# A new order for the splits at the border between the value product and the attention heads

## The chip, the cores and the metric

The kernel runs on one core of a Trainium2 chip. The metric is device time in microseconds (us), lower is better; the time of a kernel is the median of its timed runs. TensorE (PE) multiplies matrices, VectorE (DVE), ScalarE (ACT) and GpSimd (POOL) work on rows of 128 partitions, and SyncE (SP) issues the transfers from device memory.

## The reference

Two residual layers over 512 frames of 1024 channels, all in float32. Layer 0 mixes by causal pooling, layer 1 by chunked attention with 16 heads of 64 channels; each is followed by a gated MLP of width 2816 with a causal convolution. What matters here is the attention of layer 1, cut to its core:

```python
qkv = h @ w_qkv
q, k, v = jnp.split(qkv, 3, axis=-1)
q = head_rmsnorm(q.reshape(B, S, N_HEADS, HEAD_DIM), q_norm)
k = head_rmsnorm(k.reshape(B, S, N_HEADS, HEAD_DIM), k_norm)
...
s = jnp.einsum('bqhd,bkhd->bhqk', qc, kb) * scale + bias
s = jnp.where(valid, s, -1e30)
p = jax.nn.softmax(s, axis=-1)
o = jnp.einsum('bhqk,bkhd->bqhd', p, vb)
return o @ w_o
```

## The kernel before

Every float32 product is made of three products of a rounded "hi" part and the "lo" rest of each operand: hi by hi, hi by lo, lo by hi. So each operand is split first: ScalarE rounds a tile to its hi part (`nc.scalar.activation(hi, raw, AF.Copy)`), and VectorE, or GpSimd for some weights, subtracts (`lo = raw - hi`).

`opening` is the first part of attention. It computes the query and key columns of the first four pairs of heads (`query`), and then the values V (512 frames by 1024 channels) by a scheme of seven block products in place of eight (Strassen's). Each of the seven has two halves, `half(0)` to `half(13)`; half n multiplies by a weight block whose parts are made by `hi(n)` (ScalarE, line 990) and `lo(n)` (VectorE, line 993). The results gather in banks of PSUM: the pair A (tiles `va0`, `va1`, in the Q banks), the pair B of the last block product but one (`vd0`, `vd1`, in the P banks), and C (`vc0`, `vc1`). Quadrants of V are sums over these banks: `add(y5, C)` and `add(y6, B)` (line 1162, two VectorE additions of 128x512 each) and, for the last, plain copies of A into `c` (`c120` on ScalarE, `c121` on VectorE). `store` then scales a finished tile of V by the norm of its frames and splits it into the tiles `one`: four ScalarE instructions (line 107) and four VectorE instructions (line 108), each 128x128.

Behind the values stands `project(1)`, the query and key columns of the next four pairs: four groups of 24 matmuls, one group for each weight tile `wqk1_0` to `wqk1_3`, each matmul triple going to one of four banks in turn. Its tiles `qk1_0` and `qk1_1` lie in the P banks, where B was, and `qk1_2` and `qk1_3` in the Q banks, where A was. So its first triple may start when `vd0` was added up, the seventh matmul when `c120` was copied, and the tenth when `c121` was copied. The first weight tile is loaded and split ahead (`then`, the split lines `nc.scalar.activation(then[0], ...)` and `nc.vector.tensor_sub(then[1], ...)`); the lo parts of the other three (`wqk1_1_l` to `wqk1_3_l`) are made by GpSimd (line 103), and their hi parts by ScalarE (line 102).

The heads follow: `scores`, `turn` and `mix` for 16 heads by four frame tiles, with the matmuls of `project` and of the output product as fillers between them.

What sets the order: in `opening` the order of PE, VectorE, ScalarE and SP is the order in which the code stands (a manual schedule). GpSimd's order, and the order of VectorE, ScalarE and SP in the heads, come from a scheduler that works with a cost model; PE's order there is written out too. Each engine works off its queue in order, so an instruction that waits holds all that stand behind it on that engine.

Of the kernel before, what the change touches and what calls it, by code (L numbers as in the profile page):

```python
# [72 lines left out]
def trunk(ctx: ExitStack, tc: tile.TileContext, xt, xT, cols, band, edge, poolw, gv, wout, wqk, wv, wo, rel, out):  # L73
# [15 lines left out]
    def psum(tag, name, bufs=2):  # L89
        return ps.tile([P, S], F32, name=name, tag=tag, bufs=bufs)  # L90
# [3 lines left out]
    def g_tile(name):  # L94
        return tmp.tile([P, S], F32, name=name, tag="g", bufs=6)
# [9 lines left out]
    def split_scaled(src, scale, hi, lo):  # L105

        nc.scalar.activation(hi, src, AF.Copy, scale=scale)
        nc.vector.scalar_tensor_tensor(lo, src, scale, hi.bitcast(F32), op0=OP.mult, op1=OP.subtract)
# [24 lines left out]
    def rsqrt(a, y, t):  # L133

        nc.scalar.activation(t, a, AF.Ln)
        seed = nc.scalar.activation(y, t, AF.Exp, scale=-0.5)
        nc.vector.scalar_tensor_tensor(t, y, -0.5, y, op0=OP.mult, op1=OP.mult)
        nc.vector.tensor_mul(t, t, a)
        return seed, nc.vector.scalar_tensor_tensor(y, t, 1.5, y, op0=OP.add, op1=OP.mult)
# [775 lines left out]
    def attention(rest, hook, hidden_slots):  # L915
# [8 lines left out]
        def norms_of(c):  # L924
            return [big.tile([P, 8 * TT], F32, name=f"qk{c}_{v}", tag="nw", bufs=4) for v in "sayt"]

        def by_frame(v):
            return v.rearrange("p (t h) -> p t h", t=TT)
# [3 lines left out]
        def opening(pre):  # L932
# [55 lines left out]
            def part_hi(key):  # L988
                part[key] = [wp.tile([P, 1024], F32R, name=f"{key}_{c}", tag=f"w{c}", bufs=2) for c in "hl"]
                nc.scalar.activation(part[key][0], raws[key], AF.Copy)  # L990

            def part_lo(key):
                nc.vector.tensor_sub(part[key][1], raws[key], part[key][0].bitcast(F32))
# [25 lines left out]
            def hi(n):  # L1019
                z, j = divmod(n, 2)  # L1020
                raws[f"v{n}"] = blocks[SEQ[z], j]
                part_hi(f"v{n}")

            def lo(n):
                part_lo(f"v{n}")
# [57 lines left out]
            def half(n, o, name, first):  # L1083
                z, j = divmod(n, 2)
                h, l = part.pop(f"v{n}")
                how = {"skip_group_check": not first}
                for c in range(2):
                    s = slice(c * S, (c + 1) * S)
                    for i in range(2):
                        sh, sl = stationary(name, 2 * j + c, i)  # L1090
                        nc.tensor.matmul(o[i], sh, h[:, s], start=first and n % 2 == 0 and c == 0, stop=False, **how)
                        nc.tensor.matmul(o[i], sl, h[:, s], start=False, stop=False, **how)
                for i in range(2):
                    for c in range(2):
                        sh, _ = stationary(name, 2 * j + c, i)
                        nc.tensor.matmul(o[i], sh, l[:, c * S:(c + 1) * S], start=False, stop=j == 1 and c == 1, **how)
# [63 lines left out]
            def add(x, o):  # L1160
                for i in range(2):
                    nc.vector.tensor_add(x[i], x[i], o[i])

            def store(src, t, h):
                for hh in range(2):
                    V[t, 2 * h + hh] = vt = set1[(t * 2 + h) * 2 + hh].rearrange("p (h a d) -> p h a d", h=4, a=2)
                    v4 = src[:, hh * 256:(hh + 1) * 256].rearrange("p (h d) -> p h d", d=HD)
                    for e in range(2):
                        split_scaled(v4[:, e::2, :], rcol[:, t:t + 1], vt[:, e::2, e, :], vt[:, e::2, 1 - e, :])

            def pair_of(name):
                return [vx(f"{name}{i}") for i in range(2)]
# [26 lines left out]
            B = [psum("P", f"vb{i}") for i in range(2)]  # L1199
# [22 lines left out]
            y6 = pair_of("y6")  # L1222
# [23 lines left out]
            y5 = pair_of("y5")  # L1246
# [3 lines left out]
            B = [psum("P", f"vd{i}") for i in range(2)]  # L1250
# [3 lines left out]
            hi(12)  # L1254
            lo(12)
            add(y5, C)
            store(y5[0], 2, 1)
            half(11, B, "a22", True)
            hi(13)
            lo(13)  # L1260
            nc.scalar.activation(then[0], raw, AF.Copy)
            add(y6, B)
            nc.vector.tensor_sub(then[1], raw, then[0].bitcast(F32))
            half(12, A, "s4", False)
            store(y5[1], 3, 1)
            half(13, A, "s4", False)
            c = pair_of("c12")
            nc.scalar.activation(c[0], A[0], AF.Copy)
            nc.vector.tensor_copy(c[1], A[1])  # L1269
            second = project(1, ready=then)  # L1270
            for _ in range(24):
                next(second)
# [6 lines left out]
        def products(ov, w, name, eng=None, evict=None, ready=None):  # L1279

            for kk in range(4):
                hi, lo = ready if ready and kk == 0 else load_split(w[kk], 1024, f"{name}_{kk}", eng=eng)

                for c, t in [(c, t) for c in range(2) for t in range(TT)] if kk < 3 else [(c, t) for t in range(TT) for c in range(2)]:
                    k = 2 * kk + c
                    s = slice(c * S, (c + 1) * S)
                    q = slice(t * P, (t + 1) * P)
                    yield from mm3(ov[t], XS[k][:, q], XS[KD + k][:, q], hi[:, s], lo[:, s], k == 0, k == KD - 1)
                    if kk == 3 and c and evict:
                        evict(t)  # L1290

        def project(c, banks="PQ", ready=None):

            ov = [psum(banks[t // 2], f"qk{c}_{t}", BANKS[banks]) for t in range(TT)]
            ss, a, y, t_ = norms_of(c)
            s3, a3, y3 = (by_frame(v) for v in (ss, a, y))

            def squares(t):
                sq = g_tile(f"zs{c}_{t}")
                nc.scalar.activation(sq, Z[c, t].rearrange("p h d -> p (h d)"), AF.Square)  # L1300
                nc.vector.tensor_reduce(s3[:, t, :], sq.rearrange("p (h d) -> p h d", d=HD), axis=mybir.AxisListType.X, op=OP.add)


            def evict(t):
                Z[c, t] = z = zp.tile([P, 8, HD], F32, name=f"z{c}_{t}", tag="z", bufs=8)
                flat = z.rearrange("p h d -> p (h d)")
                if t % 2:
                    nc.vector.tensor_copy(flat, ov[t])
                else:
                    nc.scalar.activation(flat, ov[t], AF.Copy)  # L1310
                late.append(lambda: squares(t))

            yield from products(ov, wqk[c], f"wqk{c}", nc.gpsimd, evict, ready)

            def norms():
                nc.vector.tensor_mul(a3, s3, r2[:, :, None].to_broadcast([P, TT, 8]))
                nc.vector.tensor_scalar(a, a, EPS, None, op0=OP.add)
                rsqrt(a, y, t_)
                nc.vector.tensor_mul(y3, y3, rcol[:, :, None].to_broadcast([P, TT, 8]))
                for t in range(TT):  # L1320
                    nc.gpsimd.tensor_mul(Z[c, t], Z[c, t], y3[:, t, :, None].to_broadcast([P, 8, HD]))

            late.append(norms)
# [105 lines left out]
        with tc.tile_pool(name="pre", bufs=1, reuse_waits="tile") as pre:  # L1429
            with tc.manual_schedule(engines={ET.PE, ET.DVE, ET.Activation, ET.SP}):  # L1430
                rcol, second = opening(pre)
# [147 lines left out]
```

## Time and profile before

| | before |
| --- | --- |
| median of 3 runs | 969.64 us |
| runs | 969.39 to 969.65 us |
| the profiled execution | 969.34 us |
| its span | 967.5 us |
| PE busy | 957.4 us, 99% of the span |
| VectorE busy | 850.8 us, 88% |
| ScalarE busy | 593.7 us, 61% |
| GpSimd busy | 94.6 us, 10% |

The border lies at 430 to 450 us of the span. Rows of the timeline read: start, duration, engine, line, operation, what is written from what, how many, and in brackets how long the engine stood idle before it and what ended that. Successive instructions of an engine overlap a little, so the step from one start to the next is shorter than the duration. Buffer numbers are left out of names: `y` is any of y50 to y61, `one` any of the tiles of V, `wqk_l` any lo part.

### The profile page before, as it was taken

What the parts mean: (1) busy time and instruction counts of PE and PEld (TensorE: products, weight loads), DVE (VectorE), ACT (ScalarE), POOL (GpSimd) and SP (SyncE); (2) the same over time, 40 slices, a digit from 0 to 9 for tenths busy, and PEclk for the clock granted to TensorE, in tenths of its full rate; (3) what the DMA queues carried; (4) which work ended last, traced back from release to release, by engine and by line L of the source; (5) the groups of instructions that cost most, each with busy time, mean ns of one, the idle gap of its engine ahead of it and who ended that gap; (6) DMA issues with size and microseconds to landing.
All of it is one profiled execution on the core that took longest, in us unless ns stands there. A gap on an engine that the chain in (4) does not pass through costs nothing.

```text
span 967.5 us, 13741 instructions
## 1 busy us (share of the span) xinstructions
PE 957.4 (99%) x4958; PEld 810.7 (84%) x4958; DVE 850.8 (88%) x1521; ACT 593.7 (61%) x1023; POOL 94.6 (10%) x82
## 2 busy tenths in 40 slices
PE   8999999999999999999999999999999999999998
PEld 7788988888888888887888787888988888888886
DVE  8999999999899859895777887999999999989953
ACT  7665554655555457465898988646565565456531
POOL 2300000000000000033435442000000000000000
PEclk9999999999999999999999999999999999999999
DMA  8222332332323317024443341232333233332323
GB/s 344 75 95 71 115 111 78 120 120 81 115 78 120 103 52 290 18 66 130 121 119 99 92 119 55 100 109 80 94 114 111 80 120 111 102 102 80 113 80 111
DMA packets 38996, 103.87 MB, mean 107 GB/s; under 512 B 4464, under 2 KB 7936, under 8 KB 38928
## 3 DMA queue, kind: packets, MB, share of 16 engines
q1 hardware_dynamic: 38864, 102.95, 32.8%
q8 instruction: 39, 0.64, 0.3%
q14 instruction: 29, 0.24, 0.1%
q0 software_dynamic: 32, 0.04, 0.0%
q10 hardware_dynamic: 32, 0.00, 0.0%
HBM read 96.65 MB, written 2.14 MB: 102 GB/s over the span
## 4 chain that ended last, share of the span: by engine, by line
PE 94%; DVE 3%; ACT 2%; issue 0%; DMA 0%; DVEq 0%
PE st_m L593 11%; PE out L124 8%; PE out L123 8%; PE out L125 8%; PE st_m L595 6%; PE st_t L593 6%; PE gv L124 4%; PE gv L123 4%; PE gv L125 4%; PE qk L123 3%; PE qk L124 3%; PE qk L125 3%; PE st_t L595 3%; PE st_b L593 3%; PE tp L1407 2%; PE oo L1419 2%
## 5 line engine op out<-in xcount | busy, mean ns | idle before, releaser
L124 PE MATMUL out<-one,ow_h 128*128 128x512 f32 x224 | 88.1, 393 | 0.0
L123 PE MATMUL out<-one,ow_h 128*128 128x512 f32 x224 | 88.0, 393 | 0.0
L125 PE MATMUL out<-one,ow_l 128*128 128x512 f32 x224 | 87.9, 393 | 0.0
L829 DVE TENSOR_TENSOR X<-out,X 128x512 f32<-128x512 f32 (+1 forms) x65 | 44.0, 678 | 46.3 <-PE out L125 46.1
L593 PE MATMUL st_m<-two,g_h 128*128 128x512 f32 x240 | 75.0, 394 | 0.0
L593 PE MATMUL st_m<-h,g_h 128*128 128x512 f32 x240 | 74.1, 390 | 0.0
L392 ACT ACTIVATE ow_h<-wo_r 128x768 fp32r<-128x768 f32 (+1 forms) x56 | 44.5, 794 | 43.2 <-PE out L124 40.6
L407 DVE SCALAR_TENSOR_TENSOR c<-a,col,c 128x511 f32<-128x511 f32 (+1 forms) x76 | 56.1, 740 | 0.0
L593 PEld LDWEIGHTS st_m<-h,g_h 128*128 128x128 f32 x240 | 45.1, 188 | 10.3
L595 PEld LDWEIGHTS st_m<-two,g_l 128*128 128x128 f32 x240 | 45.0, 188 | 9.6
L602 ACT ACTIVATE w<-st_m 128x512 f32<-128x512 f32 x30 | 17.9, 598 | 56.6 <-PE st_m L595 56.6
L593 PEld LDWEIGHTS st_m<-two,g_h 128*128 128x128 f32 x240 | 44.1, 188 | 10.1 <-ACT w L602 0.8
L393 DVE TENSOR_TENSOR ow_l<-wo_r,ow_h 128x768 fp32r<-128x768 f32 (+1 forms) x56 | 49.8, 890 | 2.1 <-ACT ow_h L392 2.1
L595 PE MATMUL st_m<-h,g_l 128*128 128x256 f32 x240 | 48.3, 283 | 0.0
L595 PE MATMUL st_m<-two,g_l 128*128 128x256 f32 x240 | 47.6, 280 | 0.0
L124 PEld LDWEIGHTS out<-one,ow_h 128*128 128x128 f32 x224 | 42.4, 189 | 5.6 <-DVE one L418 0.3
L125 PEld LDWEIGHTS out<-one,ow_l 128*128 128x128 f32 x224 | 42.4, 189 | 5.5
L123 PEld LDWEIGHTS out<-one,ow_h 128*128 128x128 f32 x224 | 42.4, 189 | 5.4
L404 ACT ACTIVATE c<-a,col 128x512 f32<-128x512 f32 x38 | 30.7, 813 | 23.6 <-DVE a L751 21.9
L1397 ACT ACTIVATE sb<-sb,mx 128x128 f32<-128x128 f32 (+1 forms) x64 | 35.7, 557 | 13.2 <-DVE mx L1395 12.8
L1395 DVE CUSTOM_DVE_ANT_0 sb<-sc,B 128x128 f32<-128x128 f32 (+1 forms) x64 | 31.1, 486 | 14.4 <-PE sc L1392 11.2
L123 PE MATMUL qk<-wqk_h,two 128*128 128x512 f32 x96 | 39.9, 416 | 1.7 <-DVE c L1269 1.7
(458 smaller groups left out, 3028.1 us busy)
## 6 DMA issues: line engine op xcount, KB each, us to landing
gv_r<-gv SPq DMA_DIRECT2D x86, 512.0 KB, 4.0
wo_r<-wout SPq DMA_DIRECT2D x32, 384.0 KB, 3.1
wo_r<-wout SPq DMA_DIRECT2D x32, 320.0 KB, 2.9
wqk_r<-wqk SPq DMA_DIRECT2D x12, 512.0 KB, 3.4
b<-wv SPq DMA_DIRECT2D x8, 512.0 KB, 6.6
wo_r<-wo SPq DMA_DIRECT2D x8, 512.0 KB, 3.4
xt<-xt SPq DMA_DIRECT2D x4, 512.0 KB, 5.2
X<-xT SPq DMA_DIRECT2D x8, 256.0 KB, 7.5
```

The costliest lines, as they stand in the source:

```text
L123: yield nc.tensor.matmul(o, sh, mh, start=first, stop=False, **how)
L124: yield nc.tensor.matmul(o, sh, ml, start=False, stop=False, **how)
L125: yield nc.tensor.matmul(o, sl, mh, start=False, stop=last, **how)
L392: nc.scalar.activation(hi[:, :n], raw[:, :n], AF.Copy)
L393: return hi, lo, lambda: nc.vector.tensor_sub(lo[:, :n], raw[:, :n], hi[:, :n].bitcast(F32))
L404: nc.scalar.activation(c, a, AF.Identity, scale=cw[2], bias=cw[3])
L407: nc.vector.scalar_tensor_tensor(c[:, j:], a[:, :S - j], cw[2 - j], c[:, j:], op0=OP.mult, op1=OP.add)
L593: nc.tensor.matmul(o, hi[:, c], B[i, name], start=first and i == 0, stop=False, **how)
L595: nc.tensor.matmul(o[:, 0], lo[:, c], B[i, name][:, 0], start=False, stop=i == 3, **how)
L829: nc.vector.tensor_add(X[d][:, fs], o[:, fs], X[d][:, fs])
L1395: nc.vector.tensor_tensor_reduce(out=s_[:, :n], in0=sc[:, :n], in1=BT[h % 2][:, :n][:, ::-1], scale=1.0, scalar=3e38, op0=OP.add, op1=OP.m ...
L1397: nc.scalar.activation(s_[:, :n], s_[:, :n], AF.Exp, scale=-1.0, bias=mx[:, 0:1], accum_out=mx[:, 1:2])
```

## The change

The same instructions are issued, in another order. `hi(13)` and the split of the first weight tile of `project(1)` come before the splits of y5, `add(y6, B)` comes before `lo(13)`, the splits of `y5[0]` come behind the split of that weight tile, and those of `y5[1]` behind the copies of the last bank into `c`.

```diff
             add(y5, C)
-            store(y5[0], 2, 1)
             half(11, B, "a22", True)
             hi(13)
+            add(y6, B)
             lo(13)
             nc.scalar.activation(then[0], raw, AF.Copy)
-            add(y6, B)
             nc.vector.tensor_sub(then[1], raw, then[0].bitcast(F32))
             half(12, A, "s4", False)
-            store(y5[1], 3, 1)
+            store(y5[0], 2, 1)
             half(13, A, "s4", False)
             c = pair_of("c12")
             nc.scalar.activation(c[0], A[0], AF.Copy)
             nc.vector.tensor_copy(c[1], A[1])
+            store(y5[1], 3, 1)
             second = project(1, ready=then)
```

VectorE from the sums of y5 to the copy of the last bank, before (`v13_l` is the lo part for half 13, `wqk1_0_l` that of the first weight tile, the tiles `one` are splits of V, `c121` the copy; x2 stands for two instructions):

```order
L1162 TENSOR_TENSOR y50_4140<-y50_4140,vc0_4027 128x512
L1162 TENSOR_TENSOR y51_4141<-y51_4141,vc1_4028 128x512
L108 SCALAR_TENSOR_TENSOR one10_90<-y50_4140,n1_y_3837,one10_90 128x2x64 x2
L108 SCALAR_TENSOR_TENSOR one11_91<-y50_4140,n1_y_3837,one11_91 128x2x64 x2
L993 TENSOR_TENSOR v13_l_4190<-b22r_1_4047,v13_h_4189 128x1024
L1162 TENSOR_TENSOR y60_4021<-y60_4021,vd0_4145 128x512
L1162 TENSOR_TENSOR y61_4022<-y61_4022,vd1_4146 128x512
L1263 TENSOR_TENSOR wqk1_0_l_4150<-wqk1_0_r_4147,wqk1_0_h_4149 128x1024
L108 SCALAR_TENSOR_TENSOR one14_94<-y51_4141,n1_y_3837,one14_94 128x2x64 x2
L108 SCALAR_TENSOR_TENSOR one15_95<-y51_4141,n1_y_3837,one15_95 128x2x64 x2
L1269 COPY c121_4230<-va1_3706 128x512
```

The same place on VectorE in the changed kernel:

```order
L1162 TENSOR_TENSOR y50_4140<-y50_4140,vc0_4027 128x512
L1162 TENSOR_TENSOR y51_4141<-y51_4141,vc1_4028 128x512
L1162 TENSOR_TENSOR y60_4021<-y60_4021,vd0_4145 128x512
L1162 TENSOR_TENSOR y61_4022<-y61_4022,vd1_4146 128x512
L993 TENSOR_TENSOR v13_l_4182<-b22r_1_4047,v13_h_4181 128x1024
L1262 TENSOR_TENSOR wqk1_0_l_4150<-wqk1_0_r_4147,wqk1_0_h_4149 128x1024
L108 SCALAR_TENSOR_TENSOR one10_90<-y50_4140,n1_y_3837,one10_90 128x2x64 x2
L108 SCALAR_TENSOR_TENSOR one11_91<-y50_4140,n1_y_3837,one11_91 128x2x64 x2
L1268 COPY c121_4222<-va1_3706 128x512
```

Ahead of the copy stand four splits of V where eight stood; the other four follow it. The sums of y6 stand ahead of `v13_l`.

ScalarE from the hi part for half 13 on, in the changed kernel (`wqk1_1_h` and `wqk1_2_h` are hi parts of the second and third weight tile, `sb0_0` the first softmax row of the heads):

```order
L990 ACTIVATE v13_h_4181<-b22r_1_4047 128x1024
L1261 ACTIVATE wqk1_0_h_4149<-wqk1_0_r_4147 128x1024
L107 ACTIVATE one10_90<-y50_4140,n1_y_3837 128x2x64 x2
L107 ACTIVATE one11_91<-y50_4140,n1_y_3837 128x2x64 x2
L102 ACTIVATE wqk1_1_h_4313<-wqk1_1_r_4312 128x1024
L1267 ACTIVATE c120_4221<-va0_3705 128x512
L107 ACTIVATE one14_94<-y51_4141,n1_y_3837 128x2x64 x2
L107 ACTIVATE one15_95<-y51_4141,n1_y_3837 128x2x64 x2
```

Before, the rows of `one10` and `one11` stood ahead of `v13_h`, and those of `one14` and `one15` ahead of `wqk1_1_h` and `c120`. After these come the splits of y6 and of `c`, 16 ScalarE instructions. `wqk1_2_h` stood ahead of the last four of them and stands behind all of them now, still ahead of the first softmax row. GpSimd takes the lo part of that tile two rows later, behind the two small memsets of the heads' tiles B:

```order
 L103 TENSOR_TENSOR wqk_1_l<-wqk_1_r,wqk_1_h 128x1024
-L103 TENSOR_TENSOR wqk_2_l<-wqk_2_r,wqk_2_h 128x1024
 L1436 MEMSET B_4306 64x64
 L1436 MEMSET B_4307 64x64
+L103 TENSOR_TENSOR wqk_2_l<-wqk_2_r,wqk_2_h 128x1024
```

Here `wqk_1_l` is `wqk1_1_l` and `wqk_2_l` is `wqk1_2_l`. The orders of PE and SP are unchanged.

## The prediction

> **What bounds the kernel now.** I read the busy times on the profile's page first, then the list of PE's waits over the whole span, and then the windows around the border.
>
> ```profile
> PE 957.4 (99%) x4958; PEld 810.7 (84%) x4958; DVE 850.8 (88%) x1521; ACT 593.7 (61%) x1023; POOL 94.6 (10%) x82
> ```
>
> ```profile
> PE qk L123 <- DVE c L1269: 1.7, 1, 1.7
> PE wo L124 <- DVE two L103: 0.6, 1, 0.6
> PE oo L1419 <- DVE pt1l L103: 0.5, 1, 0.5
> ```
>
> ```profile
> 420.00:440.00 20.00, 19.82 (x88) 15.69 (x86) 19.36 (x29) 16.00 (x36) 4.38 (x3) 1.00 0.42 125
> 440.00:460.00 20.00, 18.44 (x85) 15.35 (x86) 9.74 (x31) 9.11 (x23) 7.36 (x5) 1.00 0.35 111
> 460.00:480.00 20.00, 20.00 (x110) 16.81 (x109) 15.57 (x47) 17.29 (x42) 10.33 (x9) 1.00 0.40 111
> ```
>
> PE bounds the kernel, and its longest single wait of the span is at the border that the change touches: 1.7 us, ended by the VectorE copy into `c`. The columns of the windows are length, PE, PEld, DVE, ACT, POOL (busy us and instructions), clock, DMA share and GB/s. VectorE is full until 440 (19.36 of 20) and half empty after it (9.74 of 20), and from 460 PE is full again: what PE wins at the border should stay won, since VectorE catches up right behind it. The clock column is 1.00 on both sides of the stall.
>
> The timeline of PE shows the loss in full.
>
> ```profile
> 437.30 0.39 PE L123 MATMUL qk<-wqk_h,two 128*128 128x512 f32 x1
> 437.77 0.50 PE L124 MATMUL qk<-wqk_l,two 128*128 128x512 f32 x1
> 439.51 0.40 PE L125 MATMUL qk<-wqk_h,two 128*128 128x512 f32 x1
> 441.56 0.50 PE L123 MATMUL qk<-wqk_h,two 128*128 128x512 f32 x1 [1.66 <-DVE c L1269]
> 441.89 0.39 PE L124 MATMUL qk<-wqk_l,two 128*128 128x512 f32 x1
> 445.10 0.39 PE L123 MATMUL qk<-wqk_h,two 128*128 128x512 f32 x1
> 450.79 0.40 PE L123 MATMUL qk<-wqk_h,two 128*128 128x512 f32 x1
> ```
>
> These are matmuls 1, 2, 9, 10, 11, 25 and 49 of `project(1)`. From 11 to 25 the step is 3.21 / 14 = 0.229 us. Without any stall, matmul 11 would stand at 437.30 + 10 x 0.229 = 439.59; it stands at 441.89. So 2.30 us are lost: a little at matmul 2, which needs `wqk1_0_l`, and the rest at matmul 10, which needs the copy `c121`. **2.30 us is the most that the change can win here.**
>
> **Why the copy is late** is read from the VectorE timeline.
>
> ```profile
> 430.05 1.22 DVE L993 TENSOR_TENSOR v_l<-b22r,v_h 128x1024 fp32r<-128x1024 f32 x1
> 431.18 1.28 DVE L1162 TENSOR_TENSOR y<-y,vc 128x512 f32<-128x512 f32 x2
> 432.38 1.18 DVE L108 SCALAR_TENSOR_TENSOR one<-y,n_y,one 128x128 fp32r<-128x128 f32 x4
> 434.16 1.23 DVE L993 TENSOR_TENSOR v_l<-b22r,v_h 128x1024 fp32r<-128x1024 f32 x1 [0.59 <-ACT v_h L990]
> 435.30 1.28 DVE L1162 TENSOR_TENSOR y<-y,vd 128x512 f32<-128x512 f32 x2
> 436.50 1.22 DVE L1263 TENSOR_TENSOR wqk_l<-wqk_r,wqk_h 128x1024 fp32r<-128x1024 f32 x1
> 437.63 3.27 DVE L108 SCALAR_TENSOR_TENSOR one<-y,n_y,one 128x128 fp32r<-128x128 f32 x4
> 440.83 0.68 DVE L1269 COPY c<-va 128x512 f32<-128x512 f32 x1
> 441.43 4.32 DVE L108 SCALAR_TENSOR_TENSOR one<-y,n_y,one 128x128 fp32r<-128x128 f32 x8
> 445.68 2.18 DVE L108 SCALAR_TENSOR_TENSOR one<-c,n_y,one 128x128 fp32r<-128x128 f32 x8
> ```
>
> VectorE is behind by its own work, and it loses 0.59 us waiting for `v13_h`. The group of four splits at 437.63 took 3.27 us, the one at 432.38 only 1.18. Taken by line, one instruction of the slow group is the difference, and GpSimd was busy beside it:
>
> ```profile
> L108 DVE SCALAR_TENSOR_TENSOR one<-y,n_y,one x4: 340/340/2486, 437.6 to 440.6; 128x128 fp32r<-128x128 f32 x4
> 437.33 2.64 POOL L103 TENSOR_TENSOR wqk_l<-wqk_r,wqk_h 128x1024 fp32r<-128x1024 f32 x1 [13.84 <-PE va L1096]
> 442.21 2.61 POOL L103 TENSOR_TENSOR wqk_l<-wqk_r,wqk_h 128x1024 fp32r<-128x1024 f32 x1 [2.23 <-ACT wqk_h L102]
> 452.25 2.40 POOL L103 TENSOR_TENSOR wqk_l<-wqk_r,wqk_h 128x1024 fp32r<-128x1024 f32 x1 [7.01 <-ACT wqk_h L102]
> 460.57 0.68 DVE L1308 COPY z<-qk 128x512 f32<-128x512 f32 x1
> 460.35 0.61 POOL L1372 CAST z<-zh 64x512 fp32r<-64x512 f32 x1
> ```
>
> Three splits took 340 ns and one 2486 ns, from 437.63 to 440.12, when GpSimd's subtraction was through at 439.97. The same again from 442.21 to 444.82, where eight splits took 4.32 us instead of 2.18. Alone, at 452.25, GpSimd's subtraction takes 2.40. While GpSimd subtracts, a VectorE split does not advance. A VectorE copy out of PSUM does: at 460.57 it takes 0.68 us beside a busy GpSimd, as long as the copy at 440.83 alone.
>
> **The change, part by part.** No instruction is added or removed, so the sum is made of places in the queues. VectorE is unchanged up to 431.18. From there: sums of y5, 1.20 (431.18 to 432.38); sums of y6, 1.20 (435.30 to 436.50), so `v13_l` can start at 433.58; it takes 1.14 (434.16 to 435.30), so `wqk1_0_l` starts at 434.72 instead of 436.50, **1.78 us earlier**. That is the four splits of `y5[0]` moved behind (1.19) and the idle 0.59. Each start has to be allowed by others.
>
> ```profile
> 430.72 0.39 PE L1092 MATMUL vd<-v_h,two 128*128 128x512 f32 x1
> 430.95 1.07 PE L1096 MATMUL vd<-v_l,two 128*128 128x512 f32 x4
> 433.67 1.07 PE L1096 MATMUL va<-v_l,one 128*128 128x512 f32 x4
> 436.39 1.07 PE L1096 MATMUL va<-v_l,one 128*128 128x512 f32 x4
> 431.89 0.40 ACT L107 ACTIVATE one<-y,n_y 128x128 fp32r<-128x128 f32 x1 [2.45 <-DVE y L1162]
> 434.03 1.05 ACT L1261 ACTIVATE wqk_h<-wqk_r 128x1024 fp32r<-128x1024 f32 x1
> 434.98 1.26 ACT L107 ACTIVATE one<-y,n_y 128x128 fp32r<-128x128 f32 x4
> 436.15 1.05 ACT L102 ACTIVATE wqk_h<-wqk_r 128x1024 fp32r<-128x1024 f32 x1
> ```
>
> The sums of y6 read bank B, which PE closes at 430.95 + 1.07 = 432.02; they start at 432.38, so the wait that they add costs nothing, with 0.36 us to spare, and only VectorE's own row stands behind them. `v13_h` takes the buffer of `v11_h`, which PE reads last at 430.72 + 0.39 = 431.11. ScalarE idled 2.45 us until 431.89 and now makes `v13_h` from 431.15 to 432.2 and `wqk1_0_h` to 433.15, both ahead of need. PE's half 13 needs `v13_l`, through at 434.80, at 436.39 only: covered by 1.6 us.
>
> What remains is whether GpSimd's subtraction of `wqk1_1` still falls on splits ahead of the copy. It needs `wqk1_1_h` from ScalarE. That now stands behind the four splits of `y5[0]`, 433.05 to 434.3, and needs its transfer.
>
> ```profile
> 431.29 0.35 SPq L117 DMA_DIRECT2D wqk_r<-wqk  x1
> wqk_r<-wqk SPq DMA_DIRECT2D x1, 512.0 KB, 3.1
> ```
>
> Issued at 431.29 when `v12_l` is through, as before, and 3.1 us to landing: 434.4. So ScalarE splits the tile from 434.45 to 435.5, and GpSimd arrives at 435.6; its buffer has been free since PE's 433.67 + 1.07 = 434.74. Before, it arrived at 437.33, behind the hi part (436.15 + 1.05 = 437.20; the bracket names PE, one of whose matmuls ended in the same moment) and 0.83 us into VectorE's `wqk1_0_l` of 436.50; now 0.9 us into the same instruction, begun at 434.72. The whole pattern is moved as it stands: **GpSimd again falls on the four splits ahead of the copy**, which now belong to `y5[0]`. From the start of `wqk1_0_l` to the copy it was 440.83 - 436.50 = 4.33 us; so the copy starts at 434.72 + 4.33 = 439.05, and PE's matmul 10 follows 0.73 after it as before (441.56 - 440.83): 439.78, against 439.36 without any stall. Matmul 11 comes 0.33 later at 440.11 instead of 441.89. The small stall at matmul 2 goes too, since `wqk1_0_l` is through at 435.94, but that only lengthens the wait at matmul 10. **Sum: -1.78 us.**
>
> Bounds: the unknown is GpSimd's hold on VectorE ahead of the copy. If it falls elsewhere, four free splits take 1.19 us, the copy waits for PE alone (436.39 + 1.07 = 437.46), and all 2.30 us are won. If it gets in before `wqk1_0_l`, that lo part is through only at about 435.94 + 2.40 = 438.34, PE's matmul 2 waits for it from 437.53 to about 438.4, and matmul 11 stands at 438.4 + 9 x 0.229 = 440.5, later than by the copy: 1.4 us are won. I take 1.78, the row at hand.
>
> The Trainium skill, page "SBUF — State Buffer", section "Who interferes with whom", says that VectorE instructions with two inputs in SBUF and GpSimd instructions that read SBUF exclude each other, and whoever starts first holds the port for its whole instruction. Taken literally, GpSimd would run 2.40 us from the end of `wqk1_0_l` and the four splits only then, 435.94 + 2.40 + 1.19 = 439.53 for the copy, a gain of 1.30 us instead of 1.78. In this trace the blocked split ends 0.15 us behind GpSimd, and less than that time is lost.
>
> Behind the border: `wqk1_2_h` stands behind all ScalarE splits. From `c120` at 437.1 + 0.57 come 20 of them at 0.29 (1.17 for four, 434.98 to 436.15), to 443.5, so `wqk1_2_h` is ready at 444.5 and GpSimd's lo part at about 447.2, against 444.82 before. Matmul 49 and 50 need it, at 450.79 - 1.78 = 449.0 and 449.2. Margin 2.0 us: nothing. It blocks the last VectorE splits to about 447.6; the first scores are wanted after 448: nothing. The hi parts ahead of it on ScalarE serve V, first needed by `mix` much later.
>
> **The rivals.**
>
> A, GpSimd is out of the way and the stall goes whole: 969.64 - 2.30 = 967.3. For it: a copy out of PSUM isn't blocked, so a `wqk1_1_h` later by 1.3 us would do. Against: transfer and ScalarE row above leave it nothing to wait for.
>
> B, GpSimd's hold lasts longer or begins before `wqk1_0_l`: gain 1.3 to 1.4, 968.3. For it: the arrival is reckoned to 0.2 us only. Against: it cannot come before 434.74, and in the rows before the four splits were through 3.20 us after their start. The skill's rule above gives this time too.
>
> C, most of the gain is given back in the heads, by small waits there that double (0.6 at `wo`, 0.5 at `oo`): 969.64 - 1.78 + 1.1 = 969.0. Against: everything behind 441 follows PE, so those waits should move with it.
>
> D, on the other side: `wqk1_2` comes too late. If ScalarE's 20 splits went at VectorE's pace in the rows above (3.20 + 4.25 + 2.18 = 9.63 from one start to the next), `wqk1_2_h` would be through at 437.67 + 9.63 + 1.05 = 448.35; if then eight VectorE splits (2.18) also went ahead of GpSimd's 2.40, the lo part would be ready at 452.9, and PE would wait from 449.2: 969.64 - 1.78 + 3.7 = 971.6. It costs from 449.2 on, and is slower than before from 451.0. Against: ScalarE's four splits take 1.26 us and wait for no one in these rows.
>
> **How the numbers follow.** Forecast 0.62, A 0.20, B 0.08, C 0.06, D 0.04. The profiled execution would take 969.34 - 1.78 = 967.56 us; runs stand 0.3 above it, so the median is 969.64 - 1.78 = **967.86 us**. A measurement of this kernel tells a change from none at about 0.2%, 1.94 us, and the forecast lies just inside. Faster by more: nearly all of A and a third of the forecast's own scatter (small waits of a few tenths in the heads), 0.39; within: 0.57; slower: 0.04. The range takes in A and B with that scatter and reaches just past C: 966.9 to 969.2.
>
> **What would show it.** Right: the wait of PE at `qk` falls from 1.66 to about 0.3 us, the copy starts near 439.05, one split of `y5[0]` again lasts about 2.5 us, matmul 11 stands near 440.1, and 460 to 480 is full on PE. A shows no wait at `qk`, B one of `qk` for `wqk_l`, D one at matmul 49 or 50. Wrong altogether: a new wait of PE between 427 and 437, where half 11 to half 13 run without a gap now.

## The result

| | before | changed |
| --- | --- | --- |
| median of 12 runs | 969.64 us | 967.72 us |
| runs | 969.24 to 970.45 us | 967.46 to 968.66 us |
| profiled execution (span) | 969.34 (967.5) us | 967.76 (966.0) us |

The ratio is 0.9982, with a 95% interval of 0.9974 to 0.9989: 1.9 us faster, clear of no change by the interval, and just inside 0.2%. The forecast was 967.86.

PE's longest waits over the whole span, in the changed kernel:

```profile
PE warm L199 <- POOL ident masks.py:199: 1.4, 1, 1.4
PE y L278 <- ACT two L222: 1.0, 1, 1.0
PE wo L124 <- DVE two L103: 0.7, 1, 0.7
PE oo L1419 <- DVE pt1l L103: 0.5, 1, 0.5
...
PE qk L123 <- DVE c L1268: 0.4, 1, 0.4
```

The wait for the copy fell from 1.7 to 0.4 us. Those in the heads, at `wo` and `oo`, are what they were to 0.1 us (0.6 and 0.5 before). The wait at `warm`, ahead of the first matmul, is 1.4 us in both kernels. The wait at `y`, at the kernel's start and untouched, happened to be 1.0 us in this execution, against 0.6 in that of before; so the spans differ by 1.5 us only, and all times at the border stand some 0.2 us later than they would.

The timeline of PE in the changed kernel, matmuls 1, 2, 9, 10, 11 and 50 of `project(1)`:

```profile
437.49 0.39 PE L123 MATMUL qk<-wqk_h,two 128*128 128x512 f32 x1
437.72 0.39 PE L124 MATMUL qk<-wqk_l,two 128*128 128x512 f32 x1
...
439.31 0.39 PE L125 MATMUL qk<-wqk_h,two 128*128 128x512 f32 x1
440.05 0.50 PE L123 MATMUL qk<-wqk_h,two 128*128 128x512 f32 x1 [0.36 <-DVE c L1268]
440.39 0.39 PE L124 MATMUL qk<-wqk_l,two 128*128 128x512 f32 x1
...
449.51 0.39 PE L124 MATMUL qk<-wqk_l,two 128*128 128x512 f32 x1
```

A measure that does not depend on where the border stands in the span is the distance from matmul 1 to matmul 11: 441.89 - 437.30 = 4.59 us before, 440.39 - 437.49 = **2.90 us** after, and 2.29 at PE's own step. It is used for every experiment below.

VectorE, and below it ScalarE and GpSimd, in the same kernel:

```profile
431.45 1.28 DVE L1162 TENSOR_TENSOR y<-y,vc 128x512 f32<-128x512 f32 x2
432.64 1.28 DVE L1162 TENSOR_TENSOR y<-y,vd 128x512 f32<-128x512 f32 x2
433.83 1.23 DVE L993 TENSOR_TENSOR v_l<-b22r,v_h 128x1024 fp32r<-128x1024 f32 x1
434.97 1.22 DVE L1262 TENSOR_TENSOR wqk_l<-wqk_r,wqk_h 128x1024 fp32r<-128x1024 f32 x1
436.11 3.29 DVE L108 SCALAR_TENSOR_TENSOR one<-y,n_y,one 128x128 fp32r<-128x128 f32 x4
439.32 0.68 DVE L1268 COPY c<-va 128x512 f32<-128x512 f32 x1
```

```profile
431.35 1.06 ACT L990 ACTIVATE v_h<-b22r 128x1024 fp32r<-128x1024 f32 x1 [1.69 <-PE vd L1092]
434.87 1.06 ACT L102 ACTIVATE wqk_h<-wqk_r 128x1024 fp32r<-128x1024 f32 x1 [0.34 <-DMA wqk_r<-wqk]
436.07 2.40 POOL L103 TENSOR_TENSOR wqk_l<-wqk_r,wqk_h 128x1024 fp32r<-128x1024 f32 x1 [12.31 <-ACT wqk_h L102]
444.72 2.78 POOL L103 TENSOR_TENSOR wqk_l<-wqk_r,wqk_h 128x1024 fp32r<-128x1024 f32 x1 [0.99 <-ACT wqk_h L102]
```

VectorE runs from the sums to the copy without a gap. ScalarE's hi part `wqk1_1_h` (434.87) waits for its transfer, as reckoned, GpSimd begins at 436.07, and the four splits beside it take 3.29 us where four free ones take 1.2.

### The profile page after: what moved, and what is told of

It reads as the page before. It is cut to its first block, busy times and chain, and to the rows that moved or that the text cites. A ratio compares the mean times of both kernels' runs of the same rounds, so it can differ in the third digit from the quotient of the medians.

```text
span 966.0 us, 13739 instructions
## 1 busy us (share of the span) xinstructions
PE 956.8 (99%) x4958; PEld 810.6 (84%) x4958; DVE 848.5 (88%) x1521; ACT 593.3 (61%) x1023; POOL 94.6 (10%) x82
## 4 chain that ended last, share of the span: by engine, by line
PE 93%; DVE 5%; ACT 1%; issue 0%; DMA 0%; DVEq 0%
PE st_m L593 11%; PE out L124 8%; PE out L125 8%; PE out L123 8%; PE st_m L595 6%; PE st_t L593 6%; PE gv L124 4%; PE gv L125 4%; PE gv L123 4%; PE qk L123 3%; PE qk L124 3%; PE qk L125 3%; PE st_t L595 3%; PE st_b L593 3%; PE tp L1407 2%; PE oo L1419 2%
## 5 line engine op out<-in xcount | busy, mean ns | idle before, releaser
L392 ACT ACTIVATE g_h<-sa 128x1024 fp32r<-128x1024 f32 x32 | 33.8, 1057 | 12.0 <-DVE sa L638 7.3
```

The costliest lines, as they stand in the source:

```text
L392: nc.scalar.activation(hi[:, :n], raw[:, :n], AF.Copy)
```

## The experiments

Theory: the rest of the stall, 0.6 us, is GpSimd's hold on the four splits ahead of the copy; and the gain depends on where GpSimd's subtraction falls, more than on how many splits stand ahead of the copy. Rivals: only VectorE's row of work counts; or GpSimd holds any VectorE instruction, the copy too.

| kernel | matmul 1 to 11, us | median, us | ratio to before (95%) |
| --- | --- | --- | --- |
| before | 4.59 | 969.64 | |
| changed | 2.90 | 967.72 | 0.9982 (0.9974 to 0.9989) |
| splits of both y5 behind the copies | 2.27 | 967.19 | 0.9974 (0.9964 to 0.9984) |
| changed, second weight tile split later | 2.26 | 967.06 | 0.9973 (0.9963 to 0.9983) |
| before, only y5[1] behind the copies | 6.19 | 970.84 | 1.0006 (0.9997 to 1.0015) |
| the same, second weight tile split later | 2.73 | 967.56 | 0.9979 (0.9970 to 0.9988) |
| changed, sums of y6 put back | 4.97 | 971.29 | 1.0012 (1.0003 to 1.0021) |
| before, two idle additions | 5.25 | 971.45 | 1.0014 (1.0005 to 1.0023) |
| before, four idle additions | 5.81 | 972.07 | 1.0024 (1.0014 to 1.0033) |

Each ratio is taken against runs of the kernel before on the same chip in the same session (medians 969.56 for the first four experiments, 969.69 for the last three). The distances are those of one profiled execution each; 6.19 and 5.25 contain matmuls at a lowered clock, of which more below.

### No split ahead of the copy

Edit to the changed kernel:

```diff
             half(12, A, "s4", False)
-            store(y5[0], 2, 1)
             half(13, A, "s4", False)
             c = pair_of("c12")
             nc.scalar.activation(c[0], A[0], AF.Copy)
             nc.vector.tensor_copy(c[1], A[1])
+            store(y5[0], 2, 1)
             store(y5[1], 3, 1)
```

> The changed kernel with the splits of y5[0] behind the copies of the last bank too, so that no split stands between wqk1_0_l and the copy c121 on VectorE. Theory (GpSimd's subtraction holds up VectorE splits, not copies out of PSUM): GpSimd still arrives about 0.9 us into wqk1_0_l, but the copy then waits for PE alone and starts about 437.5 on the clock of the trace before; PE has no wait at qk; matmul 11 of project(1) starts 2.3 us behind matmul 1 (4.59 before, 2.90 in the changed kernel); 0.6 us under the changed kernel, about 967.2 us. Rival (GpSimd holds VectorE whatever it does): the copy is held until GpSimd ends at about 438.2 or blocked for 2.4 us, and matmul 11 stays at 2.9 us or more, 967.7 us or slower.

```profile
435.16 1.21 DVE L1262 TENSOR_TENSOR wqk_l<-wqk_r,wqk_h 128x1024 fp32r<-128x1024 f32 x1
437.86 0.69 DVE L1267 COPY c<-va 128x512 f32<-128x512 f32 x1 [1.49 <-PE va L1096]
436.16 2.47 POOL L103 TENSOR_TENSOR wqk_l<-wqk_r,wqk_h 128x1024 fp32r<-128x1024 f32 x1 [12.22 <-ACT wqk_h L102]
437.66 0.39 PE L123 MATMUL qk<-wqk_h,two 128*128 128x512 f32 x1
439.93 0.39 PE L124 MATMUL qk<-wqk_l,two 128*128 128x512 f32 x1
```

The copy waits for PE and runs from 437.86 to 438.55 in the middle of GpSimd's 436.16 to 438.63, at its usual 0.69 us. PE does not wait: matmul 11 (439.93) stands 2.27 us behind matmul 1. So the copy out of PSUM is not held, and the rival by which GpSimd holds everything falls. The row of before at 460.57 could not show this: the copy there ran beside a GpSimd cast of 0.61 us, not beside the subtraction.

### The hold taken away, the four splits left

Edit to the changed kernel, which splits the second weight tile right behind the ScalarE copy:

```diff
             nc.scalar.activation(c[0], A[0], AF.Copy)
+            next_ = load_split(wqk[1, 1], 1024, "wqk1_1", eng=nc.gpsimd)
             nc.vector.tensor_copy(c[1], A[1])
             store(y5[1], 3, 1)
-            second = project(1, ready=then)
+            second = project(1, ready=(then, next_))
...
-                hi, lo = ready if ready and kk == 0 else load_split(w[kk], 1024, f"{name}_{kk}", eng=eng)
+                hi, lo = ready[kk] if ready and kk < 2 else load_split(w[kk], 1024, f"{name}_{kk}", eng=eng)
```

> The changed kernel with the split of the second weight tile wqk1_1 written behind the ScalarE copy c120, so that GpSimd's subtraction begins about 438.8 instead of 436; the four splits of y5[0] stay ahead of the copy c121. Theory (the hold on those four splits is the whole rest of the stall): the four splits take 1.2 us instead of 3.3, no wait of PE at qk, matmul 11 at 2.3 us behind matmul 1, about 967.2 us; the hold falls on splits behind the copy. Rival (VectorE's own row of work ahead of the copy is too long even without the hold): matmul 11 stays near 2.9 us, 967.7 us.

```profile
435.86 1.13 DVE L108 SCALAR_TENSOR_TENSOR one<-y,n_y,one 128x128 fp32r<-128x128 f32 x4
437.42 0.69 DVE L1269 COPY c<-va 128x512 f32<-128x512 f32 x1 [0.44 <-PE va L1096]
438.83 5.25 DVE L108 SCALAR_TENSOR_TENSOR one<-y,n_y,one 128x128 fp32r<-128x128 f32 x12 [0.72 <-ACT one L107]
438.64 2.40 POOL L103 TENSOR_TENSOR wqk_l<-wqk_r,wqk_h 128x1024 fp32r<-128x1024 f32 x1 [15.15 <-ACT wqk_h L102]
```

The same four splits take 1.13 us instead of 3.29, VectorE then idles 0.44 us for PE, and PE's distance is 2.26. The hold, 2.40 us long, now falls on splits behind the copy, where twelve take 5.25 us, and costs PE nothing. By its median, 967.06 us, this is the fastest kernel of the study, though 0.13 us under the last one is not clear of noise.

### Fewer splits ahead of the copy, GpSimd a little earlier

Edit to the kernel before, the smallest that puts four splits fewer ahead of the copy:

```diff
             half(12, A, "s4", False)
-            store(y5[1], 3, 1)
             half(13, A, "s4", False)
...
             nc.vector.tensor_copy(c[1], A[1])
+            store(y5[1], 3, 1)
             second = project(1, ready=then)
```

> The kernel before with one edit: the splits of y5[1] stand behind the copies; those of y5[0] stay where they were. ScalarE then comes to the hi part of wqk1_1 four splits sooner, and GpSimd arrives about 436.1, just ahead of VectorE's wqk1_0_l at 436.5. Theory (who comes first holds the port): wqk1_0_l is held until GpSimd ends, through at about 439.3, PE waits at matmul 2 for it instead of at matmul 10 for the copy, matmul 11 about 4.3 us behind matmul 1, gain 0.2 to 0.4 us, about 969.3 us. Rival (only the number of splits ahead of the copy counts): four splits fewer ahead of the copy, copy at about 437.7, matmul 11 at 2.6 us, gain 2.0, 967.6 us.

```profile
435.37 1.28 DVE L1162 TENSOR_TENSOR y<-y,vd 128x512 f32<-128x512 f32 x2
436.56 3.12 DVE L1263 TENSOR_TENSOR wqk_l<-wqk_r,wqk_h 128x1024 fp32r<-128x1024 f32 x1
439.61 0.68 DVE L1268 COPY c<-va 128x512 f32<-128x512 f32 x1
436.22 2.38 POOL L103 TENSOR_TENSOR wqk_l<-wqk_r,wqk_h 128x1024 fp32r<-128x1024 f32 x1 [12.67 <-ACT wqk_h L102]
```

GpSimd began 0.34 us ahead of VectorE's `wqk1_0_l`, and that instruction took 3.12 us instead of 1.22. The sums just ahead, which read one operand from PSUM, took their usual 1.28, the last 0.4 us of it beside GpSimd. The theory's place holds: PE waits at matmul 2 for `wqk1_0_l`, and the rival's 967.6 us is off by more than 3 us. Its time does not hold: it was to be 969.3 and is 970.84, which by the interval is no gain, and the distance is 6.19 us and not 4.3. Some 0.4 us of the difference is `wqk1_0_l`, through at 439.68 where 439.3 was expected. The rest is not on VectorE:

```profile
437.30 0.39 PE L123 MATMUL qk<-wqk_h,two 128*128 128x512 f32 x1
439.74 0.68 PE L124 MATMUL qk<-wqk_l,two 128*128 128x512 f32 x1 [2.05 <-DVE wqk_l L1263]
440.22 0.63 PE L125 MATMUL qk<-wqk_h,two 128*128 128x512 f32 x1
440.64 0.63 PE L123 MATMUL qk<-wqk_h,two 128*128 128x512 f32 x1
...
443.20 0.44 PE L123 MATMUL qk<-wqk_h,two 128*128 128x512 f32 x1
443.49 0.40 PE L124 MATMUL qk<-wqk_l,two 128*128 128x512 f32 x1
```

In the windows view the next to last three columns of a row are the clock, the DMA share and GB/s:

```profile
437.30:439.70 2.40, 0.39 (x2) 0.00 (x0) 2.40 (x2) 2.40 (x9) 1.39 (x2) 1.00 0.32 123
439.70:443.20 3.50, 3.46 (x8) 2.73 (x9) 3.50 (x13) 3.50 (x13) 0.00 (x0) 0.53 0.67 221
443.20:446.00 2.80, 2.80 (x13) 2.31 (x12) 2.34 (x9) 1.23 (x2) 0.00 (x0) 0.98 0.60 189
```

After a PE wait of 2.05 us the granted clock was 0.53 for 3.5 us, and the eight steps from 439.74 to 443.20 took 0.43 us each instead of 0.23: (3.46 - 8 x 0.229) = 1.6 us lost on top of the wait. Of the 11 executions six have a mean clock of 0.998 over the span and 970.84 to 971.11 us; five have 1.0 and 969.18 to 969.91. Where the clock was kept, this kernel is about as fast as before (median 969.69), without the gain of 0.2 to 0.4 us expected.

### The same with the hold taken away

The edit of the last kernel and that of the one before it together, on the kernel before.

> The same as the kernel before with only the splits of y5[1] behind the copies, and the split of wqk1_1 behind the ScalarE copy c120, so that GpSimd arrives about 438.8, behind the copy c121. Theory: wqk1_0_l and the copy are free, PE waits 0.2 us for wqk1_0_l at matmul 2, matmul 11 at about 2.6 us behind matmul 1, gain 2.0 us against before, 967.6 us: 1.6 us or more under the same kernel without the later split. Rival (the hold does not matter): the same time as that kernel.

Measured: matmul 1 to 11 in 2.73 us, 967.56 us, ratio 0.9979. `wqk1_0_l` again takes 1.22 us, the copy follows at once, and PE waits 0.17 us for `wqk1_0_l`. Between this kernel and the last one the order of VectorE, PE and GpSimd is the same; only the place of one ScalarE instruction, `wqk1_1_h`, and with it GpSimd's start (436.22 against 439.01), differs. That is worth 3.3 us between the medians, and 2.1 against the executions of the last kernel that kept the clock.

### Only the splits moved

Edit to the changed kernel:

```diff
             hi(13)
-            add(y6, B)
             lo(13)
             nc.scalar.activation(then[0], raw, AF.Copy)
+            add(y6, B)
             nc.vector.tensor_sub(then[1], raw, then[0].bitcast(F32))
```

> The changed kernel with the sums of y6 put back behind lo(13) and the first weight tile's hi part, so that only the splits of y5 (and with them the hi parts) have moved. VectorE's row ahead of the copy is as long as in the changed kernel; but the order in which the scheduler builds the rest comes out different at one place: ScalarE's wqk1_2_h stands ahead of the copy c120, and GpSimd's second subtraction follows its first at once. Theory (holds by GpSimd ahead of the copy set the end): the second subtraction begins about 438.5 and holds two more splits of y5[0] for 2.4 us, the copy starts about 441.4, PE waits more than 2 us at matmul 10, and most or all of the gain is gone: 969.5 us or more, up to 971.5 if the wait costs PE its clock as in the kernel with only y5[1] moved. Rival (the moved splits alone carry the gain, wherever GpSimd works): 967.7 us as the changed kernel.

```profile
435.91 1.22 DVE L1262 TENSOR_TENSOR wqk_l<-wqk_r,wqk_h 128x1024 fp32r<-128x1024 f32 x1
437.04 5.40 DVE L108 SCALAR_TENSOR_TENSOR one<-y,n_y,one 128x128 fp32r<-128x128 f32 x4
442.36 0.68 DVE L1268 COPY c<-va 128x512 f32<-128x512 f32 x1
437.02 5.00 POOL L103 TENSOR_TENSOR wqk_l<-wqk_r,wqk_h 128x1024 fp32r<-128x1024 f32 x2 [12.34 <-ACT wqk_h L102]
443.10 0.50 PE L123 MATMUL qk<-wqk_h,two 128*128 128x512 f32 x1 [2.32 <-DVE c L1268]
```

`wqk1_0_l` starts 2.55 us ahead of matmul 1 (438.46), as in the changed kernel (2.52): on VectorE the place of the sums is worth nothing. But the scheduler now put ScalarE's `wqk1_2_h` ahead of `c120`, GpSimd did two subtractions in a row, and four splits took 5.40 us. The gain is gone: 4.97 us from matmul 1 to 11 where the clock was kept (as in the profiled execution), and 971.06 us or more in the seven executions of 11 with a mean clock of 0.998. The rival falls: the moved splits do not carry the gain by themselves.

### Longer waits of PE

Two idle VectorE additions ahead of the copy (four in the second kernel), on the kernel before; they compute nothing that is used. (With four, and in the kernel with only the splits moved, the scheduler also put four transfers of the heads, tiles `B`, behind one of a weight tile.)

```diff
             nc.scalar.activation(c[0], A[0], AF.Copy)
+            idle = pre.tile([P, P], F32, name="idle", tag="idle", bufs=1)
+            for _ in range(2):
+                nc.vector.tensor_add(idle, y5[0][:, :P], y5[1][:, :P])
             nc.vector.tensor_copy(c[1], A[1])
```

> The kernel before with two idle VectorE additions of 128x128 ahead of the copy c121 (their result is used by nothing), so that PE's wait at matmul 10 grows from 1.66 to about 2.2 us; nothing else is changed. Theory (a PE wait of some 2 us can cost the clock: after the 2.05 us wait of the kernel with only y5[1] moved, the granted clock was 0.53 for about 3.5 us): some of the executions show a granted clock of 0.998 and 1.6 us more; they lie near 970.1 and near 971.7 us. Rival (the low clock there had another cause, such as the wait falling on matmul 2 or the transfers beside it): all executions near 970.1 us.

> The same with four idle additions, wait about 2.8 us. Theory, form one (a fixed length of idling between 1.66 and 2.05 us takes the clock): every execution shows the low clock, about 972.3 us. Form two (the longer the wait, the likelier, as with a window that runs on its own): a larger share of executions than with two additions, at 972.3, the others near 970.7 us. Rival: no execution, 970.7 us.

With two additions PE waited 2.22 us and lost its clock in the profiled execution; seven executions of 11 lie at 971.41 to 972.54 us with a mean clock of 0.997 or 0.998, four at 969.88 to 970.65 with 0.999 or 1.0. With four, PE waited 2.86 us and the profiled execution kept its clock (its 972.00 us contain a wait of 1.1 us at `y`, at the kernel's start); six of nine have 0.998 (972.06 to 973.01). So a wait at matmul 10 loses the clock too: the place at matmul 2 is not needed. Transfers ran beside all these waits, but also beside the 1.66 us of the kernel before (DMA share 0.70 from 438.82 to 442.23), where the clock was kept; so they alone are not the cause. A fixed length of the wait (form one) falls: 2.05 us lost the clock and 2.86 us kept it.

What decides it can be read from the traces. The low clock lasts one step of 3.41 us (439.89 to 443.30 with only y5[1] moved, 442.72 to 446.13 with two additions). The clock falls again behind the last matmul, at 968.96 and 968.37, and that is 155 and 154 such steps after the first fall (3.4133 us each). So it changes on a grid of its own. The two fences show the steps around the wait, counted back from the fall behind the last matmul: first with only y5[1] moved and with two additions, then with only the splits of y5 moved (wait of 2.32 us) and with four additions.

```profile
436.48:439.89 3.41, 1.36 (x7) 0.82 (x6) 3.41 (x3) 2.84 (x10) 2.21 (x2) 1.00 0.41 148
439.89:443.30 3.41, 3.41 (x9) 2.67 (x10) 3.41 (x13) 3.41 (x13) 0.00 (x0) 0.50 0.72 235
...
439.31:442.72 3.41, 1.19 (x6) 0.69 (x5) 3.38 (x9) 3.41 (x10) 1.18 (x2) 1.00 0.82 263
442.72:446.13 3.41, 3.41 (x9) 2.63 (x9) 3.41 (x6) 1.02 (x4) 2.33 (x2) 0.50 0.34 115
```

```profile
439.09:442.50 3.41, 1.69 (x7) 0.88 (x6) 3.41 (x4) 3.41 (x12) 3.02 (x3) 1.00 0.70 249
442.50:445.91 3.41, 2.81 (x12) 2.36 (x13) 3.41 (x13) 3.12 (x11) 0.00 (x0) 1.00 0.66 227
...
439.61:443.02 3.41, 1.69 (x8) 1.03 (x6) 3.34 (x7) 3.41 (x12) 1.78 (x1) 1.00 0.67 195
443.02:446.44 3.42, 2.28 (x10) 1.90 (x11) 3.39 (x6) 1.80 (x5) 2.47 (x2) 1.00 0.30 115
446.44:449.85 3.41, 3.41 (x17) 2.83 (x16) 3.41 (x14) 0.00 (x0) 0.14 (x1) 1.00 0.79 224
```

The first number behind the length is PE's busy time. Where the wait lay whole in one step, PE was idle for 3.41 - 1.36 = 2.05 and 3.41 - 1.19 = 2.22 us of it, and the next step had half the clock. Where an edge cut the wait (1.72 and 0.60 us, 1.72 and 1.14), the clock was kept, though the whole wait was longer. In the nine traces there is no exception: after the 11 steps in which PE was idle for 2.03 us or more (these two and nine around the last matmul) the clock was low, and after the 2524 in which it was idle for 1.73 us or less it was full. No run moves the grid on purpose, so this is read from traces and not tested.

That longer waits lose the clock more often is not shown by the counts: six of 11 at 2.05, seven of 11 at 2.22 and at 2.32, six of nine at 2.86 are shares too close to tell. They fit the grid, which is the window that form two supposed: if its place is left to chance, a limit of 1.73 or of 2.03 us within a step would give 28 or 21 of these 42 executions (an estimate from the lengths above), and 26 were counted. In the 52 executions of the kernel before that ran beside these experiments, with its wait of 1.66 us, no mean clock is under 0.999.

## Why the prediction was right

**The bound.** 2.30 us were to be won at most. The two kernels without a wait at the border stand 2.26 and 2.27 us from matmul 1 to 11, 2.33 and 2.32 under before, and won 2.5 and 2.4 us between medians, 0.1 to 0.2 us more than the bound, about the scatter of these medians.

**VectorE's row.** `wqk1_0_l` was to start 1.78 us earlier. Against matmul 1 it moved from 0.80 to 2.52 us ahead: 1.72. The sums did not wait, the idle 0.59 is gone, and `v13_h` started at 431.35 as PE let its buffer go.

**GpSimd falls on the four splits again.** It was to arrive 0.9 us into `wqk1_0_l`. ScalarE waited for the transfer, GpSimd began 1.10 us into it, and the copy came 4.35 us behind its start, where 4.33 was taken from before. The step on which the size of the gain rested held to 0.02 us, and two experiments show that its cause is right: with the hold away the last 0.6 us come too.

The arrival was 0.2 us later than reckoned, which cost nothing, since GpSimd still began 0.04 us ahead of the first split (436.07 against 436.11). That it gets in there at all was taken from rows of the kernel before, not reasoned, and it is not always so: its second subtraction in the changed kernel (444.72) came while VectorE was splitting `c`; the eight splits took their usual 2.18 us, and GpSimd took 2.78 us where 2.40 is its own time. With the second weight tile split later it took 3.05 us in the same place. What decides which of the two waits stays open, so in this part the forecast had luck.

**The literal reading of the Trainium skill.** By the rule of the Trainium skill, page "SBUF — State Buffer", section "Who interferes with whom", the copy would have come 4.81 us behind `wqk1_0_l` (439.53 - 434.72). The trace has 4.35, so the row was the better price. The exclusion itself holds wherever the two met: a VectorE instruction with two operands in SBUF and GpSimd's subtraction each time made one of the two take longer (VectorE 3.12 us for 1.22, GpSimd 3.05 for 2.40). A copy or a sum that reads PSUM was not held.

**Behind the border.** `wqk1_2_l` was to be ready at 447.2 with a margin of 2.0 us; it was ready at 444.72 + 2.78 = 447.50 and matmul 50 came at 449.51. That it would block VectorE's last splits did not come true (GpSimd waited, as said above), and this cost nothing. PE's waits in the heads are unchanged to 0.1 us, and from 460 to 480 PE is full (20.00 of 20), so nothing was given back.

**The sum.** 1.78 us forecast, 1.69 between matmuls 1 and 11, 1.92 between the medians. The profiled executions differ by 1.58, since this one lost more at the start.

**What was missing.** No rival had PE's clock in it. Forecast and rivals A to C shorten the wait, where it plays no part; but the rivals' list took a wait for its own length, and from 2.05 us on it could cost 1.6 us more. Rival B, GpSimd ahead of `wqk1_0_l`, was priced at a gain of 1.4 us with the changed row; in the one kernel where that happened, with another row, matmul 1 to 11 became longer (6.19 us, some 4.6 of it without the lowered clock, where 4.59 stood before).

## What to carry to other kernels

A stall on a PSUM bank is cured by the place of one copy in one queue, but look at what stands ahead of that copy on the other engine too: here the place of one GpSimd subtraction of 2.4 us, ahead of the copy or behind it, was worth 2.1 us between two kernels (clock kept in both), as much as the whole reordering. Read a VectorE instruction that is suddenly several times its usual length as a wait, and look what GpSimd did beside it; the copy and the sums with an operand in PSUM were not held in these runs. A PE wait of 2 us or more can cost more than its length; up to 1.7 us none took the clock here. And after every edit compare the order on all engines: a line whose own place is worth nothing can make a scheduler move something that is.

## What the runs showed that was not expected

A PE wait of 2.05 to 2.86 us can take PE's clock to half, for 3.41 us, and cost 1.6 us beyond the wait: granted clock 0.50 from 439.89 to 443.30, steps of 0.43 us instead of 0.23. It happened in 26 of 42 executions of the four kernels with such waits (6 of 11, 7 of 11, 7 of 11, 6 of 9, counted by a mean clock of 0.998 or less over the span; two of the 26 were profiled and show the place), and it did not in the executions of the kernel before, with 1.66 us. The medians of executions with and without it lie 1.3, 1.5 and 1.4 us apart in the first three of these kernels, and 0.5 in the last, where only three kept the clock; so 1.6 is the figure of one trace. What counts in the traces is not the wait but PE's idle time within one step of a 3.41 us grid: 1.73 us kept the clock, 2.03 lost it. The Trainium skill, page "TensorE: Matmul & The Clock Gate", section "Why this matters for your kernels", advises against PE gaps of more than about 3 us; here gaps of 2.05 us were enough in some executions, and the measurement decides. The Trainium skill, in Part 1 of that page, has the activity window run on its own, not from the kernel's start; the traces agree, with steps of 3.41 us whose edges fall elsewhere against the wait in each of them.

A VectorE instruction that is held shows as a long instruction, not as idle time, and so the idle columns of the groups do not show it.
